# The second layer's down product computed as 15 products of block sums, with the sums of weights formed among keys and queries and the sums of activations formed in DRAM

## The chip, the cores and the metric

The kernel runs on one core of a Trainium2 chip. The metric is the device time of one launch in microseconds (us). The core has TensorE for matrix products (PE in the profile, with PEld for its weight loads), VectorE (DVE), ScalarE (ACT), GpSimd (POOL) and SyncE (SP), each with its own queue that runs in order, and 16 DMA engines that move data between DRAM and the on-chip memory. SP, ACT and POOL issue the DMAs.

## The reference

One inference step of a two-layer decoder over 1104 rows: 64 sample rows, 16 meta rows and 1024 prompt rows. The first layer mixes with an mLSTM, the second with a forgetting attention that reads one shared set of keys and values. Each layer ends with a SwiGLU feed-forward block, and this is the part that the change touches in the second layer:

```python
def swiglu(xn, w_gu, w_d):
    gu = xn @ w_gu
    return (jax.nn.silu(gu[..., :D_FF]) * gu[..., D_FF:]) @ w_d
...
h = h + swiglu(rmsnorm(h, prm['norm_ffn'][l]), prm['w_gate_up'][l], prm['w_down'][l])
```

The model width is 1024 and `D_FF` is 2816, which is 22 blocks of 128. All data is float32.

## The kernel before, in words

**Tiling.** Activations lie transposed, features on the 128 partitions and rows along the free axis, in three groups of rows `TS` of 336, 384 and 384 (`t` = 0, 1, 2; `SL` = 384 is the widest). A float32 operand is split into a high and a low part (`split`, L338 on ScalarE and L339 on VectorE), and a product is three matmuls, high·high, high·low and low·high (`mm3`, L266 to L268).

**Gate/up.** The gate/up product of both layers already runs as a scheme of 18 products and their block sums (`Unit`, L1505), one pass per 128 output columns: `Unit(x)` with even `x` makes gate values, with odd `x` up values, and the odd one multiplies them (L1524) and stores each finished 128-row block of the hidden activations to a DRAM buffer `hT[t]` from SP (L1525). Block numbers `f` run from 0 to 21; blocks 0 and 1 come from `direct`. The sums of gate/up weights are formed by POOL (`PairWeights.sums`, L108) one to two units ahead, and split by ScalarE and VectorE. In the loop over units only TensorE's order is written out by hand (`fixed()`); the other engines' order is chosen by a planner that simulates readiness.

**Down.** The loop over `seq` takes the three groups, two halves `z` of 512 output columns, and 11 pairs `c` of feature blocks: 66 steps. A step loads 256 x 512 weights from SP (`w_load`, L1629), splits them (`w_split`) and multiplies them for four output tiles `m`. Activations are loaded from `hT` by POOL (`h_load`, L1612) and split once per group and pair (`h_split`, used for both halves). Each output tile is added to the residual `H[t]` once, when its sum over all 22 blocks is done (L1480 is `add`, in this loop as in gate/up). TensorE's, VectorE's and ScalarE's order is written out here. `each` squares finished tiles for the final norm (`add_sq`; L411 on ScalarE, L413 on POOL, L639 and L641 for the last ones) and `final` transposes them (L1885), scales them (L1902) and stores the outputs.

**Keys and queries.** In `phase_b` the two projections `w_kvf` and `w_qo` are made in 256-column pieces, four each, over nine row tiles: 72 calls of `evac`, in which ScalarE copies (L2026) and squares the result and VectorE sums the squares (L2029). Three tiles later `then` scales a group (L2067) and `turn` transposes it on TensorE (L2040) and stores it from POOL (L2049). POOL also stores the keys (`out_rows`, L1989 to L1991). All orders here are the planner's.

**Queues and memory.** SP carries weight loads and the stores of `hT`; POOL's queue carries its additions and the DMAs that it issues. `order` is the hand-written order of TensorE, VectorE and ScalarE around the start of gate/up. `cw` holds the slots with gate/up weights, `cg` the tiles of gate/up alone.

## Time and profile before

| What | Value |
|---|---|
| Median of 3 runs | 2865.33 us (2863.34 to 2866.32) |
| Profiled execution, span from first to last instruction | 2855.2 us |
| TensorE busy | 2790.4 us, 98% |
| VectorE / ScalarE / GpSimd busy | 1724.8 / 1311.8 / 1018.3 us |
| Second layer's gate/up, from unit 2 | 2174 to 2572 us of the span |
| Second layer's down | 2572 to 2845 us |
| Keys and queries | 1378 to 1591 us |

For the profiled execution the span is the only time at hand; the runs' times are some 10 us longer, as they hold what lies before the first and after the last instruction. In the rows that follow, a group line gives the line of the kernel, engine, operation, output and inputs with their shapes and the count, then busy time and mean ns of one, then the idle time of the engine just before, and what ended most of it. A wait line gives who waited for whom: total us, times, the longest. A DMA line gives the issuing queue, count, size and median us from issue to landing.

### The profile page before, as it was taken

What the parts mean: (1) busy time and instruction counts of PE and PEld (TensorE: products, weight loads), DVE (VectorE), ACT (ScalarE), POOL (GpSimd) and SP (SyncE); (2) the same over time, 40 slices, a digit from 0 to 9 for tenths busy, and PEclk for the clock granted to TensorE, in tenths of its full rate; (3) what the DMA queues carried; (4) which work ended last, traced back from release to release, by engine and by line L of the source; (5) the groups of instructions that cost most, each with busy time, mean ns of one, the idle gap of its engine ahead of it and who ended that gap; (6) DMA issues with size and microseconds to landing.
All of it is one profiled execution on the core that took longest, in us unless ns stands there. A gap on an engine that the chain in (4) does not pass through costs nothing.

```text
span 2855.2 us, 53625 instructions
## 1 busy us (share of the span) xinstructions
PE 2790.4 (98%) x20485; PEld 2671.0 (94%) x20485; DVE 1724.8 (60%) x3478; ACT 1311.8 (46%) x2622; POOL 1018.3 (36%) x1495
## 2 busy tenths in 40 slices
PE   7999999999999999999999999999999999999999
PEld 7998989999999999999999888777999999999999
DVE  6044555887787755553355443777478777765553
ACT  6132464444444434443344544878244444443432
POOL 3022333075556311115352202554307656531210
PEclk9999999999999999999999999999999999999999
DMA  7057655132222275544443676442412222237652
GB/s 214 19 145 175 165 160 180 48 91 76 79 84 78 95 269 198 205 144 133 149 165 129 243 282 222 156 141 87 161 60 87 79 74 84 74 102 251 221 186 99
DMA packets 312444, 400.19 MB, mean 140 GB/s; under 512 B 28143, under 2 KB 235051, under 8 KB 311163
## 3 DMA queue, kind: packets, MB, share of 16 engines
q1 hardware_dynamic: 277234, 277.79, 30.7%
q0 software_dynamic: 33728, 118.38, 12.7%
q8 instruction: 161, 2.64, 0.4%
q10 hardware_dynamic: 1224, 0.60, 0.1%
q14 instruction: 97, 0.79, 0.1%
HBM read 299.92 MB, written 96.77 MB: 139 GB/s over the span
## 4 chain that ended last, share of the span: by engine, by line
PE 71%; DVE 9%; issue 4%; ACT 3%; DMA 2%; POOL 1%; DVEq 0%; ACTq 0%; SPq 0%; POOLq 0%
PE m L1505 24%; PE dps L266 6%; PE dps L268 6%; PE dps L267 6%; PE tmps L266 3%; PE tmps L268 3%; PE tmps L267 3%; PE sp L2597 2%; DVE slot L339 2%; PE pops L268 1%; PE pops L266 1%; PE pops L267 1%; PE op L2693 1%; PE bps L266 1%; DVE s L2606 1%
## 5 line engine op out<-in xcount | busy, mean ns | idle before, releaser
L339 DVE TENSOR_TENSOR slot<-slot,slot 128x1024 fp32r<-128x1024 f32 (+3 forms) x263 | 266.4, 1015 | 129.9 <-ACT slot L338 123.6
L338 ACT CAST slot<-slot 128x1024 fp32r<-128x1024 f32 (+3 forms) x263 | 206.8, 788 | 229.3 <-PE dps L267 91.3
L1505 PE MATMUL m<-x1h,slot 128*128 128x384 f32 x640 | 178.0, 338 | 2.4 <-DVE vA L1480 0.8
L1505 PE MATMUL m<-x0h,slot 128*128 128x336 f32 x640 | 167.0, 316 | 0.0
L413 POOL TENSOR_TENSOR ns<-ns,nq 128x384 f32<-128x384 f32 (+1 forms) x59 | 63.9, 1083 | 208.8 <-ACT nq L411 207.6
L1505 PE MATMUL m<-x2h,slot 128*128 128x384 f32 x480 | 135.8, 337 | 0.0
L1612 POOL DMA_DIRECT2D hr<-hT x60 | 32.6, 543 | 283.1 <-DVE T_2l L339 69.6
L108 POOL TENSOR_TENSOR slot<-Ht 128x256 f32<-128x256 f32 x80 | 74.9, 946 | 151.3 <-DMA Ht<-in_w_gate_up 147.0
L108 POOL TENSOR_TENSOR slot<-vA 128x256 f32<-128x256 f32 x80 | 74.2, 937 | 151.5 <-DMA vA<-in_w_gate_up 147.8
L339 DVE TENSOR_TENSOR slot<-Ht,slot 128x256 fp32r<-128x256 f32 (+3 forms) x101 | 84.8, 841 | 63.7 <-ACT slot L338 63.7
L339 DVE TENSOR_TENSOR slot<-vA,slot 128x256 fp32r<-128x256 f32 (+3 forms) x101 | 85.7, 850 | 61.7 <-ACT slot L338 61.7
L1505 PEld LDWEIGHTS m<-x1h,slot 128*128 128x128 f32 x640 | 117.1, 188 | 3.4 <-DVE vA L1480 1.2
L1505 PEld LDWEIGHTS m<-x0h,slot 128*128 128x128 f32 x640 | 113.3, 188 | 0.0
L1505 PE MATMUL m<-x1l,slot 128*128 128x384 f32 x320 | 107.8, 337 | 0.0
L1505 PE MATMUL m<-x0l,slot 128*128 128x336 f32 x320 | 101.0, 316 | 0.0
L1505 PE MATMUL m<-T_2h,slot 128*128 128x384 f32 x320 | 97.1, 344 | 3.0 <-ACT Ht L1511 0.9
L2629 ACT ACTIVATE s<-s,nb 128x272 f32<-128x272 f32 (+7 forms) x126 | 98.9, 787 | 0.2 <-POOL nb L2620 0.2
L1505 PE MATMUL m<-T_4h,slot 128*128 128x384 f32 x320 | 95.9, 340 | 0.0
L2664 ACT COPY th<-tp 128x768 f32<-128x768 f32 (+1 forms) x80 | 73.6, 921 | 46.4 <-PE tp L2656 25.9
L108 POOL TENSOR_TENSOR Ht<-Ht 128x512 f32<-128x512 f32 (+1 forms) x60 | 84.5, 1409 | 28.4 <-DVE wl1l L339 28.4
L108 POOL TENSOR_TENSOR vA<-vA 128x512 f32<-128x512 f32 (+1 forms) x60 | 84.5, 1409 | 27.5 <-DVE wl0l L339 27.5
L2029 DVE TENSOR_REDUCE ss<-sqb 128x4 f32<-128x256 f32 (+1 forms) x72 | 30.2, 419 | 101.3 <-ACT sqb L2028 100.4
(838 smaller groups left out, 10267.7 us busy)
## 6 DMA issues: line engine op xcount, KB each, us to landing
slot<-in_w_down SPq DMA_DIRECT2D x88, 512.0 KB, 4.4
wr<-in_w_down SPq DMA_DIRECT2D x42, 512.0 KB, 4.5
wraw<-in_w_in_a SPq DMA_DIRECT2D x40, 512.0 KB, 4.0
vA<-in_w_gate_up SPq DMA_DIRECT2D x40, 512.0 KB, 4.0
Ht<-in_w_gate_up SPq DMA_DIRECT2D x40, 512.0 KB, 4.1
hr<-hT POOLq DMA_DIRECT2D x46, 384.0 KB, 5.2
kp<-in_cache_k SPq DMA_DIRECT2D x32, 512.0 KB, 6.2
vp<-in_cache_v SPq DMA_DIRECT2D x32, 512.0 KB, 7.4
```

The lines of the kernel that those rows point to most:

```text
L108: self.net.nc.gpsimd.tensor_tensor(out=o, in0=a, in1=b, op=op)
L266: mm(ps, sh, mh, start=first, stop=False)
L267: mm(ps, sh, ml, start=False, stop=False)
L268: mm(ps, sl, mh, start=False, stop=last)
L338: self.nc.scalar.copy(hi, src)
L339: self.nc.vector.tensor_tensor(out=lo, in0=src, in1=hi.bitcast(F32), op=ALU.subtract)
L413: (nc.vector if x >= late else nc.gpsimd).tensor_tensor(out=s, in0=s, in1=sq, op=ALU.add)
L1505: nc.tensor.matmul(u.b[b][:, :n], w[p][:, k], x[q][:, k], start=new and k == i == 0, stop=k == 1 and i == 2, skip_group_check=True)
L1612: nc.gpsimd.dma_start(hraw[j], hT[t][:, 2 * c : 2 * c + 2])
L2597: nc.tensor.matmul(ps[z][:, :n], a[r, qs], b[r, at : at + n], start=(y == 0), stop=(y == 2))
L2629: nc.scalar.activation(ss[z, u], ss[z, u], AF.Exp, bias=nb[:, z : z + 1], accum_out=sm[:, u, z : z + 1])
L2664: nc.scalar.copy(th.rearrange("p x z (u h q) -> p h (x z u) q", h=2, q=64)[:, :, :n], pt[:, :, :n])
```

## The change

The hidden activations' first 21 blocks are taken as a 3 x 3 grid: three groups `k` of 7 feature blocks by three groups `t` of rows. The weights' first 21 blocks are a 3 x 2 grid: `k` by the two output halves `z`. The product of the two grids, 18 block products, is formed as 15 products, each of a signed sum of weight blocks with a signed sum of activation blocks, whose results are added to or subtracted from several output blocks. The 22nd block (`last`) is multiplied plainly inside some of them. The first layer keeps its down product (`plain`, now in `plain_down`).

- *Weights.* 4 of the 15 products read `w_down` as it is (`RAW`), 11 read sums (`MADE`) that `combine` forms in 14 rounds of loads (SP), additions (VectorE) and stores to DRAM (POOL). `evac` of keys and queries calls it one step at a time.
- *Activations.* `h_out` stores a finished block to all DRAM buffers that begin with it (`FIRST`), `h_minus` negates some tiles on ScalarE and stores them again (`MINUS`), and `h_add` adds one buffer to another by an accumulating DMA within DRAM that POOL issues (`ACCUMULATE` by unit, `LATER` for the last three blocks). In gate/up of the second layer POOL's order is now written out by hand too.
- *Down.* 62 steps of one or two blocks; each loads weights and activations (SP, the first five from POOL), splits both, and multiplies. A product's results stay in the four accumulators, the next may add to them with the fitting sign, and `evict` adds the state after a product to each output block that it names. Loads run eight steps ahead, splits three.
- *Around it.* Gate/up's tiles and weight slots are freed before down, whose tiles take their place; residuals are read back in halves at fixed steps; squares with index 4 and up are summed by VectorE in place of POOL; `order` is closed after the second of four parts of unit 2, in both layers.

```diff
+RAW = {1: (0, 0), 3: (0, 2), 5: (1, 0), 6: (1, 1)}
+MADE = (2, 11, 7, 12, 9, 8, 13, 10, 14, 4, 15)
+ACTS = {1: ("s1", 1), 2: ((1, 0), 1), 3: ("s3", 1), 4: ((1, 1), 1), 5: ("s5", 1), 6: ("s6", 1), 7: ("s7", -1),
+        8: ("s8", 1), 9: ("s9", 1), 10: ((0, 2), 1), 11: ("s11", -1), 12: ((2, 0), 1), 13: ("s13", 1), 14: ((0, 1), 1),
+        15: ((2, 2), 1)}
+FIRST = {(0, 0): ("s1", "s5"), (0, 1): ((0, 1), "s13", "s11"), (0, 2): ((0, 2), "s8"), (1, 0): ((1, 0),),
+         (1, 1): ((1, 1), "s3", "s9"), (1, 2): ("s6",), (2, 0): ((2, 0),), (2, 1): ((2, 1),), (2, 2): ((2, 2),)}
+MINUS = {(1, 0): "n10", (1, 2): "s7", (2, 0): "n20", (2, 1): "n21"}
+LATER = (("s5", "n20"), ("s13", (2, 0)), ("s3", (2, 0)), ("s11", "n21"), ("s9", (2, 2)), ("s3", (2, 1)), ("s11", (2, 2)),
+         ("s6", (2, 2)))
+ACCUMULATE = {9: (("s1", (0, 1), 0, 4), ("s5", (0, 2), 0, 4)), 11: (("s1", (0, 1), 4, 7), ("s5", (0, 2), 4, 7)),
+              15: (("s8", (1, 0), 0, 4), ("s6", (1, 0), 0, 4), ("s8", (1, 0), 4, 7)),
+              16: (("s6", (1, 0), 4, 7), ("s7", (0, 2), 0, 4), ("s1", "n10", 0, 4)),
+              17: (("s7", (0, 2), 4, 7), ("s7", (1, 1), 0, 4)), 18: (("s1", "n10", 4, 7), ("s7", (1, 1), 4, 7)),
+              19: tuple((a, b, 0, 4) for a, b in LATER[:4]), 20: tuple((a, b, 0, 4) for a, b in LATER[4:])}
+DOWN = ((2, 1, ((0, 0, 1),), None, True), (8, -1, ((0, 2, -1),), None, False), (10, 1, ((1, 2, 1),), None, False),
+        (5, -1, ((1, 0, -1),), (1, 0), False),
+        (12, 1, ((1, 0, 1), (1, 1, -1)), None, True), (14, 1, ((0, 1, 1),), None, False),
+        (1, -1, ((0, 0, -1),), (0, 0), False),
+        (13, 1, ((0, 0, 1),), None, True), (3, -1, ((0, 1, -1),), None, False), (11, 1, ((1, 1, 1),), (1, 1), False),
+        (4, 1, ((0, 2, 1),), None, True), (0, 1, ((0, 1, 1),), (0, 1), False),
+        (9, 1, ((0, 2, 1), (1, 1, 1)), None, True),
+        (15, 1, ((1, 1, -1),), None, True), (0, -1, ((1, 2, -1),), (1, 2), False),
+        (6, 1, ((1, 2, 1),), None, True), (7, -1, ((0, 2, -1),), (0, 2), False))
...
+                def each(t, m, x):
+                    if cb or t < 2 or x < KT - 2:
+                        self.add_sq(H, t, m, sp, x, KT - 1 if cb else 4)
...
+        def h_put(o, x, j):
+            n = min(hT[x].shape[2], o.shape[1])
+            nc.sync.dma_start(hT[x][:, j, :n], o[:, :n])
+
+        def h_out(o, f, t, c=None):
+
+            o = o[:, : size[t]]
+            if plain:
+                return nc.sync.dma_start(hT[t][:, f], o)
+            k, j = divmod(f, 7)
+            if k == 3:
+                return h_put(o, t, 0)
+            for x in FIRST[k, t]:
+                h_put(o, x, j)
+            if (k, t) in MINUS:
+                negs.append((c, o, MINUS[k, t], j))
+
+        def h_minus(cs):
+            for y in [y for y in negs if y[0] in cs]:
+                negs.remove(y)
+                _, o, x, j = y
+                nc.scalar.activation(o, o, AF.Copy, scale=-1.0)
+                h_put(o, x, j)
+
+        def h_add(x, y, a, b):
+            n = min(hT[x].shape[2], hT[y].shape[2])
+            nc.gpsimd.dma_start(hT[x][:, a:b, :n], hT[y][:, a:b, :n], accum_op=ALU.add)
...
+        steps = []
+        for p, s, ev, last, new in DOWN:
+            js = list(range(7)) if p else []
+            s = [s * (ACTS[p][1] if p else 1), s]
+            if last:
+                js.append(NF - 1)
+            parts = [js[:1]] * (len(js) % 2) + [js[x : x + 2] for x in range(len(js) % 2, len(js), 2)]
+            for x, ts in enumerate(parts):
+                n = size[0] if p in (1, 5) or p in (2, 12) and x else SL
+                steps.append((p, [s[j > 7] for j in ts], ts, last, n, new and x == 0, ev if x == len(parts) - 1 else None))
...
+        def x_load(e=nc.sync):
+            i = len(xraw)
+            if i == len(steps) or not place["tmp"]:
+                return False
+            p, _, ts, last, n, *_ = steps[i]
+            xraw[i] = place["tmp"].pop(0)
+            js = [j for j in ts if j < 7]
+            if js:
+                y = hT[ACTS[p][0]][:, js[0] : js[-1] + 1]
+                e.dma_start(xraw[i][:, : len(js), : y.shape[2]], y)
+                if y.shape[2] < n:
+                    nc.gpsimd.memset(xraw[i][:, : len(js), y.shape[2] :], 0.0)
+            if len(js) < len(ts):
+                e.dma_start(xraw[i][:, len(js), : size[last[1]]], hT[last[1]][:, 0])
+            return True
+
...
-        order.close()
-        with fixed():
+            if g % 2:
+                order.close()
+        with fixed(*(() if plain else (E.Pool,))):
...
+                    if g == 2 and not plain:
+                        for y in ACCUMULATE.get(x, ()):
+                            h_add(*y)
+                    if g == 3:
+                        if x + 2 < NF:
+                            weights.sums(x + 2, slice(0, 9))
+                    if x % 2 == 0 and g != 2:
+                        h_minus((("s1", "v2"), ("t4", "c15"), (), ("s2", "e"))[g])
...
+        if plain:
+            return plain_down(v)
+        dn = ExitStack()
+        with fixed(E.DVE, E.Activation, E.Pool, E.SP):
...
+            tail = u.tail()
+            next(tail)
             cg.close()
...
+            cw.close()
+            dp = dn.enter_context(self.pool(f"dn{l}"))
...
+            for y in range(5):
+                (x_load if y % 2 else w_load)(nc.gpsimd)
+            for y in range(2):
+                w_split(y)
+                x_split(y)
+            w_load()
+            w_load()
+            x_load()
+            x_load()
+            for _ in tail:
+                pass
+            h_minus(fs)
+            h_add(*LATER[0], 4, 7)
...
+            h_load(0, 0, 4)
+            h_load(2, 0, 4)
+            w_split(2)
+            x_split(2)
+            while len(wraw) < 7 and w_load():
+                x_load()
...
+            loads = {3: lambda: h_load(2, 4, 8), 6: lambda: h_load(0, 4, 8),
+                     9: lambda: h_load(1, 4, 8), 12: lambda: h_load(1, 0, 4)}
...
+            def evict(ev):
+                for m in range(4):
+                    for z, t, f in ev:
+                        h = H[t][:, 4 * z + m]
+                        tt(out=h, in0=h, in1=acc[m][:, : size[t]], op=ALU.add if f > 0 else ALU.subtract)
+                for z, t, f in ev:
+                    gone[z, t] = gone.get((z, t), 0) + 1
...
+            for i, (p, s, ts, last, n, lead, ev) in enumerate(steps):
+                w, x = wpart[i], xpart[i]
                 for m in range(4):
                     if lead:
...
+                        acc[m] = bank("dps", "f" if banks in (4, 5) else "d")
+                        banks += 1
+                    for k in range(len(ts)):
+                        for q, (a, b) in enumerate(((0, 0), (0, 1), (1, 0))):
+                            c = SL if lead and k == q == 0 else n
+                            nc.tensor.matmul(acc[m][:, :c], w[a][:, k, m * P : m * P + P], x[b][:, k, :c],
+                                             start=lead and k == q == 0, stop=k == len(ts) - 1 and q == 2,
+                                             skip_group_check=True)
+                for y, r in zip(("wh", "wl", "xh", "xl"), (*w, *x)):
+                    place[y].append(r)
+                if ev and (len(ts) == 1 or i == len(steps) - 1):
+                    evict(ev)
+                x_split(i + 3)
+                w_split(i + 3)
+                while len(wraw) <= i + 8 and w_load():
                     pass
+                while len(xraw) <= i + 8 and x_load():
+                    pass
+                if ev and len(ts) == 2 and i < len(steps) - 1:
+                    evict(ev)
+                if i in loads:
+                    loads[i]()
+                if i in range(4, 18, 2):
+                    h_add(*LATER[i // 2 - 1], 4, 7)
+                for _ in range(2 if p in (6, 7) else 1):
+                    next(norms, None)
+                for _ in range(99 if i == len(steps) - 1 else 2):
+                    if pend:
+                        pend.pop(0)()
+            for _ in end(fin, pp, 2):
...
+def combine(self, l, pool):
+
+    nc = self.nc
+    add = lambda o, a, b, op=ALU.add: nc.vector.tensor_tensor(out=o, in0=a, in1=b, op=op)
+    rows = self.I["w_down"][l][: 21 * P].rearrange("(k j p) n -> j p k n", k=3, p=P)
+    comb = self.dram.tile([len(MADE), 7 * P, 512], F32, name=f"wc{l}")
+    self.comb[l] = {p: comb[x] for x, p in enumerate(MADE)}
+    t = pool.tile([P, 15, 256], F32, name=f"wcs{l}")
+    w, o = t[:, :6], t[:, 6:]
+    for j in range(7):
+        for c in range(2):
+            at = lambda z: rows[j][:, :, 512 * z + 256 * c : 512 * z + 256 * c + 256]
+            put = lambda a, y: nc.gpsimd.dma_start(
+                comb[a, j * P : j * P + P, 256 * c : 256 * c + 256].rearrange("s p n -> p s n"), y)
+            nc.sync.dma_start(w[:, :3], at(0))
+            nc.sync.dma_start(w[:, 3], at(1)[:, 1])
+            nc.sync.dma_start(w[:, 4:], at(1)[:, ::2])
+            yield
+            yield
+            add(o[:, 0:2], w[:, 0:3:2], w[:, 1:6:4])
+            add(o[:, 2:4], w[:, 1:5:3], w[:, 3:6:2])
+            yield
+            add(o[:, 4], w[:, 2], w[:, 3])
+            add(o[:, 5:7], o[:, 0:2], w[:, 3:5])
+            yield
+            add(o[:, 7], o[:, 5], w[:, 4])
+            add(o[:, 8], o[:, 6], w[:, 0])
+            add(w[:, 1:4:2], w[:, 1:4:2], w[:, 2:6:3], ALU.subtract)
+            put(slice(0, 9), o)
+            put(slice(9, 11), w[:, 1:4:2])
+            yield
+
+
...
         behind = []
+        cm = ExitStack()
+        made = self.combine(1, cm.enter_context(self.pool("wcB")))
...
+                    next(made, None)
...
+        for _ in made:
+            pass
+        cm.close()
```

356 lines of the change are left out of this document (227 added, 129 removed).

## The prediction

> **What bounds the kernel now.** I read the page's busy shares and slices first, then the chain of work that ended last, then busy time by stretch for the three places that the change touches, then the groups, waits and DMA landings inside those stretches. All lines are of the kernel before.
>
> ```profile
> span 2855.2 us, 53625 instructions
> PE 2790.4 (98%) x20485; PEld 2671.0 (94%) x20485; DVE 1724.8 (60%) x3478; ACT 1311.8 (46%) x2622; POOL 1018.3 (36%) x1495
> ...
> PE   7999999999999999999999999999999999999999
> ...
> PEclk9999999999999999999999999999999999999999
> ...
> PE m L1505 24%; PE dps L266 6%; PE dps L268 6%; PE dps L267 6%; PE tmps L266 3%; PE tmps L268 3%; PE tmps L267 3%; PE sp L2597 2%; DVE slot L339 2%; PE pops L268 1%; PE pops L266 1%; PE pops L267 1%; PE op L2693 1%; PE bps L266 1%; DVE s L2606 1%
> ```
>
> TensorE is busy for 98% of the span, with a granted clock of nine tenths or more in every slice; the chain of last work is mostly its products, 24% of the span the gate/up products (L1505). Products taken away come off the time, unless something else is late where they stood. The places, one row each (PE, PEld, DVE, ACT, POOL busy with instruction counts, granted clock, DMA share, GB/s):
>
> ```profile
> 2572.00:2845.00 273.00, 273.00 (x1650) 272.73 (x1649) 132.65 (x141) 99.17 (x119) 39.34 (x50) 1.00 0.57 191
> 1378.00:1591.00 213.00, 213.00 (x1849) 213.00 (x1847) 108.97 (x255) 97.37 (x282) 85.64 (x133) 1.00 0.42 145
> 2174.00:2572.00 398.00, 395.95 (x2298) 392.51 (x2299) 301.94 (x478) 186.91 (x382) 217.71 (x217) 1.00 0.27 83
> ```
>
> First the second layer's down product, then keys and queries, then the second layer's gate/up from unit 2 on. In all three TensorE has no idle time worth a name, while VectorE is at 49%, 51% and 76% and the DMA engines at 0.57, 0.42 and 0.27 of their time. So the question is only which of the added work finds cover.
>
> **Part 1: the products removed.** Before, each of 3 token groups takes 2 output halves, 22 blocks of 128 features and 4 output tiles, three matmuls each (the split in high and low parts): 3·2·22·4·3 = 1584, one third of them 336 wide and the rest 384.
>
> ```profile
> 2575.00:2645.00 70.00, 70.00 (x457) 1.00 0.71 248
> 2660.00:2840.00 180.00, 174.93 (x993) 1.00 0.53 178
> 2572.00:2845.00 273.00, 267.66 (x1584) 1.00 0.57 191
> ```
>
> These are the same stretches for the products' own tile alone. The first holds 336-wide ones: 70.00/457 = 0.1532 us each. The second holds 384-wide ones, with the output's transposes between them: 174.93/993 = 0.1762 us. 528·0.1532 + 1056·0.1762 = 267.0, which is the third row's 267.66. After, 15 products of 7 blocks and 6 single blocks (the 22nd block, for each group and half) make 111 blocks of 12 matmuls. Products 1 and 5 are 336 wide with their 8 blocks each, 2 and 12 in all but their first block: 28 blocks narrow, 83 wide. 336·0.1532 + 996·0.1762 = 51.5 + 175.5 = 227.0. TensorE's saving is **40.0 us**; that term stands on counts and rows alone.
>
> **Part 2: weight sums among keys and queries.** Per round: three loads of 384, 128 and 256 KB on SP, seven additions of 2816 columns on VectorE, two stores of 1152 and 256 KB from POOL. There are 14 rounds, and a round advances one step after each of the 72 projections, five steps to a round.
>
> ```profile
> L2026 ACT COPY raw<-tmps x72: 353/373/377, 1379.5 to 1591.3; 128x256 f32<-128x256 f32 x64, 80x256 f32<-80x256 f32 x8
> L2029 DVE TENSOR_REDUCE ss<-sqb 128x4 f32<-128x256 f32 (+1 forms) x71 | 29.8, 419 | 101.1 <-ACT sqb L2028 100.2
> L339 DVE TENSOR_TENSOR slot<-slot,slot 128x512 fp32r<-128x512 f32 x37 | 27.2, 734 | 1.2 <-ACT slot L338 0.6
> L339 DVE TENSOR_TENSOR slot<-slot,slot 128x256 fp32r<-128x256 f32 x18 | 7.5, 419 | 0.7
> L1991 POOL DMA_DIRECT2D out_p_k<-raw x4 | 3.7, 916 | 0.4 <-issue 0.4
> slot<-in_w_qo_b SPq DMA_DIRECT2D x12, 512.0 KB, 4.4
> out_p_k<-raw POOLq DMA_DIRECT2D x4, 1024.0 KB, 5.5
> vD<-vst POOLq DMA_DIRECT2D x3, 1024.0 KB, 9.3
> POOL raw L2021 <- DMA out_p_k<-raw: 18.6, 4, 5.1
> 1600.00:1650.00 50.00, 48.97 (x541) 41.49 (x543) 21.00 (x66) 22.87 (x42) 7.32 (x13) 1.00 0.90 313
> ```
>
> VectorE: four additions of 512 columns at 734 ns and three of 256 at 419 make 4.2 us a round, 58.7 in all; 109 + 59 of 213 us is 79%, so as work it fits. DMA: 2176 KB a round, 31.2 MB in all, 146 GB/s on top of the stage's 145; the last row shows 313 GB/s moved at a share of 0.90, so this fits too, tightly. The order is what does not fit. The next round's loads overwrite rows that the second store still reads, so a round is one chain: load, add, issue, store. By rows: loads 4.9 (between 4.4 for 512 KB and 5.5 for 1024), additions 4.2 with a projection's reductions between them 5.5, two store issues on POOL 0.9 + 0.6 (the second an estimate from the first, as it is a quarter of the size), landing 6.9 (5.5 for 1024 KB alone, 9.3 for the second of two such stores issued together, hence 2048 KB; 1408 KB lies between). Sum 18.8 us. The program gives a round five projections of 213/72 = 2.96 us, 14.8. The ends: 14.7 with nothing between the additions and the nearest short landings (4.4 + 4.2 + 0.6 + 5.5), which is no delay; 22 with 9.3 us for the stores and 5.5 for the loads. Where a round is late by 4 us, VectorE's next addition waits in its queue with the reductions of later projections behind it. TensorE does not read VectorE's reductions; ScalarE empties its four banks, and VectorE sits idle for 101 us here already. But the transposes of finished groups read rows that VectorE scales, so lateness that adds up reaches TensorE there. POOL's own wait for a store in this stage (18.6 us over four, up to 5.1) cost TensorE nothing. Lower bound 0, upper 14·4.0 = 56 (100 with the longest landings every time). I take **8**, near the lower end, because the nearest row is a wait of that size that stayed free; rounds that end late run on beside the sample's attention.
>
> The Trainium skill's page "DMA: Bandwidth & Descriptors", section "Anatomy of one DMA — SWDGE (gpsimd) path", fits a transfer at 2.0 us plus bytes over 436 GB/s. By it 1408 KB land in 5.3 us and 768 KB in 3.8, the round takes 16.1, and the excess would be at most 14·1.3 = 18 us. This case's rows are slower than that fit (1024 KB: 5.5 against its 4.4), so I go by the rows.
>
> **Part 3: activation sums beside gate/up.** The stores of each finished block go to every sum that begins with it: 15 per block and 7 blocks, 28 negated copies and 3 for the last block, 136 stores instead of 66. POOL issues 30 accumulating transfers within DRAM, 22 here and 8 in the down product. ScalarE negates 28 tiles.
>
> ```profile
> hT<-Ht SPq DMA_DIRECT2D x28, 192.0 KB, 2.2
> L1527 ACT ACTIVATE ns<-ns 128x384 f32<-128x384 f32 x17 | 8.9, 524 | 27.4 <-DVE ns L1480 22.8 <-DVE ns L1481 4.6
> POOL slot L108 <- DMA Ht<-in_w_gate_up: 76.6, 17, 4.8
> hr<-hT POOLq DMA_DIRECT2D x23, 384.0 KB, 5.2
> vA<-hD POOLq DMA_DIRECT2D x4, 1536.0 KB, 9.5
> ```
>
> ScalarE: 28·0.52 = 15 us on 187 of 398. POOL: 22·0.9 = 20 us on 218, now in written order, with 76.6 us of waits for weights to absorb it. Stores: some 13 MB, 33 GB/s on 83. Each accumulation follows its blocks' stores by two units or more, so its wait is over when POOL reaches it. What is late next, if POOL is held, is the weight sums two units ahead. I take **2** (0 if POOL's waits absorb all, 20 if none). An accumulation's duration is in no row; the nearest are Pool-issued DRAM reads, 5.2 us for 384 KB and 9.5 for 1536, so 6.6 for 768 KB. The eight of units 19 and 20 would take 53 us; from their first issue to the down product's start are some 54 (a unit is 120 matmuls of 0.17 us, 21 us; 8 of unit 19, units 20 and 21, 4 of the last unit's rest).
>
> **Part 4: the start of down.** Its first five loads are issued by POOL, behind those accumulations; they wait until the gate/up operands that lay there are read. Twelve products of six matmuls stand after the last of these, 72·0.17 = 12 us, and load, cast and rest need 5 to 6. Before, TensorE goes from gate/up to down without a gap. I take **3** (0 to 27, the latter where an accumulation takes 10 us).
>
> **Part 5: down itself.** Every step now splits weights and activations: 62 steps (49 pairs, 13 single), and 76 evictions into H instead of 24, where the next product adds to the same bank.
>
> ```profile
> L339 DVE TENSOR_TENSOR slot<-slot,slot 128x1024 fp32r<-128x1024 f32 x42 | 55.9, 1334 | 49.1 <-ACT slot L338 49.1
> L339 DVE TENSOR_TENSOR x2l<-hr,x2h 128x768 fp32r<-128x768 f32 x8 | 7.6, 950 | 1.2 <-ACT x2h L338 1.2
> L1480 DVE TENSOR_TENSOR Ht<-Ht,dps 128x384 f32<-128x384 f32 x16 | 8.9, 554 | 37.7 <-PE dps L268 37.7
> L338 ACT CAST slot<-slot 128x1024 fp32r<-128x1024 f32 x41 | 43.0, 1050 | 91.6 <-PE dps L267 64.1 <-DMA slot<-in_w_down 25.0 <-PE dps L268 1.1
> L338 ACT CAST x2h<-hr 128x768 fp32r<-128x768 f32 x8 | 6.7, 833 | 2.8 <-DMA hr<-hT 2.8
> L1902 DVE SCALAR_TENSOR_TENSOR Ht<-fin,fr,gfin 128x512 f32<-128x512 f32 x16 | 11.1, 746 | 4.9 <-PE fin L1885 4.7
> SPq L1629 <- DVE slot L339: 176.5, 62, 11.8
> ```
>
> VectorE: 49·(1.33 + 0.95) + 13·(0.73 + 0.55) = 128, evictions 76·0.55 = 42, final scaling 18·0.75 = 13, squares 6 (those with index 4 and up move from POOL): 190 of 227 us, 84% where it was 49%. ScalarE: 49·(1.05 + 0.83) + 13·1.0 = 105 and 13 for squares, 52%. DMA: 29 MB of weights, 22 of activations, about the bytes of before in less time, 191·273/233 = 224 GB/s, below the 313 shown above. In a step that ends a product TensorE takes 24·0.176 = 4.2 us and VectorE 2.3 for the split and 2.2 for four evictions, 4.5; with two targets 6.7. The split runs three steps ahead, so VectorE starts early, and the excess is 0.3 at fifteen places and 2.5 at two: 9.5 at most, 0 where it starts early enough. I take **3**. SP's weight loads, which waited 176 us for free buffers, share their queue with the activations; they have eight steps' lead. That hand order ends two steps earlier in unit 2 of both layers I cost at nothing, as VectorE has 24% to spare there; if not, some 1 us a layer.
>
> **Part 6: the tail.**
>
> ```profile
> 2844.83 0.18 DVE Ht L1480
> ...
> 2845.30 0.56 DVE ns L641
> ```
>
> One eviction and one sum of squares lie between the last product and the end's scaling. Now four evictions stand ahead of the sums in VectorE's order; TensorE finishes tile by tile, so about **1** us.
>
> **Sum.** −40.0 + 8 + 2 + 3 + 3 + 1 = −23.0, against the profiled span of 2855.2: 2832. The median of the runs, 2865.3, is 10.1 above that span, which I leave as it is: 2842.
>
> **Rivals.** (a) *The round fits* (14.7 us, the lower end): keys and queries pay nothing, −31, 2834. For it: the short landings in the rows; against: 2.2 MB more each round lengthen them. Chance 0.20. It is where the page's fit, named above, points. (b) *Keys and queries run at the round's pace*, the case on the other side: the planner sets VectorE's additions by its own idea of a landing, each of 14 rounds is late by 4.0, and after one round's worth of slack (assumed) TensorE's transposes wait: 52 instead of 8, 2886. It turns the sign when the stage pays 31, at rounds of 17.3 us. For it: 18.8 against 14.8; against: TensorE's banks do not hang on VectorE. Chance 0.20. (c) *VectorE bounds down*: the excess of 9.5 comes in full, and half as much again from splits that then start late: 15 instead of 3, 2854. For it: 84%; against: three steps' lead. Chance 0.15. (d) *The accumulations are late*: at 10 us each, eight take 80 where 54 are there, so the first products wait some 27 instead of 3: 2866, no change, the case in which TensorE's saving is real and nothing comes of it. Chance 0.10, as no row shows such a transfer.
>
> **How the numbers follow.** My forecast has 0.35, (a) 0.20, (b) 0.20, (c) 0.15, (d) 0.10. A change of 0.2% (5.7 us) is about what can be told from none. Faster: forecast and (a) 0.55, (c) 0.14, (d) 0.03, (b) in part 0.02, together 0.74. Same: 0.01 + 0.03 + 0.03 = 0.07. Slower: (b) 0.15 and (d) 0.04, 0.19. Range: low end all costs at nothing, 2825; high end 2878, which leaves out most of (b). The forecast's own range is 2825 to 2855.
>
> **What the profile after would show.** Down's tile with 1332 matmuls in about 230 us; keys and queries at 213 us with TensorE without idle time and 14 rounds of additions at 4.2 us, their start 15 us apart (right) or 19 with TensorE idle before transposes (rival b); no gap at gate/up's end (d: ScalarE waiting for a DMA there); evictions that TensorE does not wait for (c: "PE waits for DVE H"). The prediction is wrong if the stretch of keys and queries grows by more than 15 us, or if a wait of SP or POOL for the accumulations ends at TensorE.

## The result and the profile after

The kernel after takes 2940.8 us (median of 5 runs, 2936.7 to 2944.5), the kernel before beside it 2863.3 us: a ratio of 1.0274, 95% interval 1.0261 to 1.0286. The change costs 2.7%. The forecast was 2842 us with a range of 2825 to 2878.

The first lines of the page, after:

```profile
span 2937.9 us, 53770 instructions
PE 2790.3 (95%) x20233; PEld 2663.9 (91%) x20233; DVE 1800.2 (61%) x3662; ACT 1327.0 (45%) x2676; POOL 1043.0 (36%) x1521
...
PE   7999989999999999999978899999999999987998
...
PEclk9999999999999999999989999999999999998999
```

TensorE is busy for as many microseconds as before (2790), although it runs 252 matmuls fewer, and for a smaller share. The row of PE now has slices at seven and eight tenths, at keys and queries (the 21st to 23rd) and about the start of down (the 36th and 37th), and PEclk has an 8 at the 21st and the 37th.

A timed run is about 2 us longer than its span, in all that are on record (2939.6 and 2937.9 for the one profiled here). The 10 us between median and profiled span of the kernel before are thus for the most part scatter: its span, 2855.2 us, is shorter than that of every timed run of that kernel on record (2855.7 to 2866.0).

The three places by stretch, in the same columns as before (us, PE, PEld, DVE, ACT, POOL busy with counts, granted clock, DMA share, GB/s): keys and queries, gate/up from unit 2, down; then the last stretch for down's tile alone (PE, PEld, DVE).

```profile
1389.00:1664.00 275.00, 234.24 (x1863) 231.94 (x1862) 156.74 (x364) 101.74 (x294) 111.37 (x163) 0.91 0.67 226
2243.00:2661.00 418.00, 400.67 (x2293) 393.74 (x2293) 291.75 (x473) 190.72 (x402) 232.23 (x240) 0.99 0.51 136
2661.00:2926.00 265.00, 242.02 (x1408) 239.71 (x1406) 169.57 (x228) 108.56 (x150) 24.56 (x24) 0.95 0.70 234
```

```profile
2661.00:2926.00 265.00, 234.06 (x1332) 230.92 (x1332) 38.38 (x76) 0.95 0.70 234
```

Keys and queries grew from 213 to 275 us and TensorE is idle for 41 of them; gate/up grew from 398 to 418 with 17 idle; down shrank from 273 to 265 only, with its 1332 matmuls as counted. For all kernels I use three stages of the profiled execution that meet without a gap: from the first copy of keys and queries to the first product of the attention's own gate behind them (`bps`; K), from there, over the attention, to gate/up's last product (G), from there to down's last product (D).

| | K | G | D |
|---|---|---|---|
| before | 216.4 | 973.9 | 274.3 |
| after | 276.0 | 996.2 | 264.5 |
| difference | +59.6 | +22.3 | -9.8 |

The other differences between the two spans (82.7 us in all) are +1.6 at the tail, +2.7 in the first layer's gate/up, +1.3 elsewhere ahead of K, and +5.0 in the first 440 us. That last part ranges from 434.2 to 440.8 us among the kernels below, none of which touches it, so it is scatter.

**Keys and queries.** Waits (who for whom, us, times, longest; `issue` is time in which nothing that the profile shows was waited for) and the landing of a round's large store, all after:

```profile
SPq L2142 <- DMA wc<-wcs: 84.2, 13, 9.7
DVE wcs L2131 <- DMA wcs<-in_w_down: 69.1, 11, 12.4
DVE wcs L2131 <- issue: 27.1, 4, 9.8
PE btp L2347 <- DVE raw L2374: 40.8, 12, 7.9
```

```profile
wc<-wcs POOLq DMA_DIRECT2D x14, 1152.0 KB, 6.6
```

SP's first load of a round waits for the store of the round before, VectorE's addition for the loads, and TensorE's transposes (`btp`) for the scaled rows (`raw`) that VectorE makes behind the additions. The rounds' first loads start 19.6 us apart in the mean, where the program has 14.8. One such wait in VectorE's order of time (start, us, instruction, and in brackets the idle time before it):

```profile
1503.62 0.42 DVE L2335 TENSOR_REDUCE ss<-sqb 128x4 f32<-128x256 f32 x1 [0.35 <-ACT sqb L2334]
1514.76 0.69 DVE L2131 TENSOR_TENSOR wcs<-wcs 128x512 f32<-128x512 f32 x1 [10.72 <-DMA wcs<-in_w_down]
1515.37 0.41 DVE L2335 TENSOR_REDUCE ss<-sqb 128x4 f32<-128x256 f32 x1
1515.70 2.42 DVE L2131 TENSOR_TENSOR wcs<-wcs 128x512 f32<-128x512 f32 x5
...
1519.72 0.95 DVE L2374 TENSOR_TENSOR raw<-raw,ss 128x768 f32<-128x768 f32 x1
```

VectorE stands 10.7 us at the first addition, and reductions and the scaling at 1519.7 come after it. What a gap does to TensorE, in stretches of 3 us:

```profile
1427.00:1430.00 3.00, 3.00 (x29) 3.00 (x28) 0.00 (x0) 0.00 (x0) 0.00 (x0) 1.00 0.88 279
1430.00:1433.00 3.00, 1.88 (x17) 1.68 (x15) 1.86 (x4) 0.74 (x4) 0.00 (x0) 1.00 0.10 36
1433.00:1436.00 3.00, 1.10 (x7) 1.13 (x7) 3.00 (x8) 0.92 (x4) 1.98 (x3) 0.68 0.32 131
1436.00:1439.00 3.00, 3.00 (x16) 3.00 (x15) 3.00 (x10) 1.55 (x4) 2.02 (x3) 0.50 0.95 324
1439.00:1442.00 3.00, 3.00 (x21) 3.00 (x20) 1.29 (x4) 0.66 (x2) 2.98 (x6) 0.68 0.97 340
1442.00:1445.00 3.00, 3.00 (x29) 3.00 (x28) 0.38 (x1) 1.01 (x4) 2.73 (x3) 1.00 1.01 349
```

TensorE is idle for 3.0 of the 6 us from 1430 to 1436, and from about 1434 to 1441 its granted clock is half (0.68 is a stretch that is part half, part full): 16 matmuls in 3 us where 29 are usual. So a wait is paid twice. Of the 59.6 us, 41 are idle time and 18 are slower products (234 us busy, where the stage's products take 216 at full clock). The Trainium skill's page "TensorE: Matmul & The Clock Gate", section "Part 1: The HAM clock gate", says that the clock is halved after an idle window of about 3.4 us and comes back after a busy one as long. The halving agrees; the slow time here, about 7 us, is longer than one such window.

**Gate/up and the start of down.** After: waits in gate/up, TensorE's wait in down and a wait of SP's queue at its start; landings from 2490 to 2660 us; down's start in stretches of 5 us; VectorE there in order of time.

```profile
ACT Ht L1542 <- DMA hT<-Ht: 37.5, 14, 6.4
PE m L1570 <- ACT ns L1576: 6.2, 6, 3.1
PE m L1570 <- ACT Ht L1576: 5.7, 8, 2.6
PE m L1570 <- ACT fs L1576: 4.4, 3, 3.0
PE dps L2098 <- DVE Ht L2079: 17.9, 2, 13.8
SPq L1523 <- ACT Ht L1542: 3.6, 1, 3.6
```

```profile
hT<-hT POOLq DMA_DIRECT2D x7, 768.0 KB, 11.8
hT<-Ht SPq DMA_DIRECT2D x18, 192.0 KB, 8.5
```

```profile
2678.00:2683.00 5.00, 3.67 (x24) 3.39 (x23) 0.00 (x0) 0.00 (x0) 0.00 (x0) 1.00 1.03 386
2683.00:2688.00 5.00, 0.00 (x0) 0.00 (x0) 2.16 (x2) 1.78 (x2) 0.00 (x0) 0.88 1.07 328
2688.00:2693.00 5.00, 0.00 (x0) 0.00 (x0) 0.27 (x1) 1.14 (x2) 0.00 (x0) 0.50 1.08 349
2693.00:2698.00 5.00, 2.54 (x8) 2.57 (x9) 5.00 (x8) 3.41 (x5) 0.00 (x0) 0.50 1.12 284
```

```profile
2685.17 0.96 DVE L1739 SCALAR_TENSOR_TENSOR dn1xl<-dn1tmp,dn1xh 128x768 fp32r<-128x768 f32 x1 [8.84 <-ACT dn1xh L1738]
2692.74 0.96 DVE L1739 SCALAR_TENSOR_TENSOR dn1xl<-x2l,dn1xh 128x768 fp32r<-128x768 f32 x1 [5.40 <-ACT dn1xh L1738]
2694.81 1.74 DVE L2079 TENSOR_TENSOR Ht<-Ht,dps 128x336 f32<-128x336 f32 x4
```

ScalarE negates in place (L1542) and must wait until the tile's first stores have been read out; these land after 8.5 us, where 2.2 were shown before. Its copies of finished products out of PSUM (L1576) stand behind it, and TensorE waits for those, 16 us in the three lines shown. At the start of down the DMA engines are full (share above 1), TensorE does nothing for some 14 us from 2682 and then starts at half clock. It waits for the first evictions (L2079); these come in VectorE's order behind two splits (L1739) for which VectorE stands 8.8 and 5.4 us, because ScalarE's casts wait for loads of activations that come late. SP's order seems to add to it (e12 below): its queue holds the last negated store (L1523), for which it waits 3.6 us, ahead of later loads of these.

### The profile page after: what moved, and what is told of

It is laid out like the page before. It is cut to its first block, busy times and chain, and to the rows that moved or that the text cites. A ratio compares the mean times of both kernels' runs of the same rounds, so it can differ in the third digit from the quotient of the medians.

```text
span 2937.9 us, 53770 instructions
## 1 busy us (share of the span) xinstructions
PE 2790.3 (95%) x20233; PEld 2663.9 (91%) x20233; DVE 1800.2 (61%) x3662; ACT 1327.0 (45%) x2676; POOL 1043.0 (36%) x1521
## 5 line engine op out<-in xcount | busy, mean ns | idle before, releaser
L365 DVE TENSOR_TENSOR slot<-slot,slot 128x256 fp32r<-128x256 f32 (+2 forms) x219 | 208.4, 953 | 84.2 <-ACT slot L364 76.6
L364 ACT CAST slot<-slot 128x256 fp32r<-128x256 f32 (+2 forms) x219 | 160.7, 735 | 151.8 <-PE m L1570 82.9
L2098 PE MATMUL dps<-dn1xh,dn1wh 128*128 128x384 f32 (+1 forms) x444 | 150.3, 339 | 20.4 <-DVE Ht L2079 17.9
L2098 PE MATMUL dps<-dn1xl,dn1wh 128*128 128x384 f32 (+1 forms) x444 | 149.3, 336 | 1.0 <-DVE dn1xl L365 1.0
L2098 PE MATMUL dps<-dn1xh,dn1wl 128*128 128x384 f32 (+1 forms) x444 | 149.1, 336 | 0.0
L365 DVE TENSOR_TENSOR slot<-Ht,slot 128x256 fp32r<-128x256 f32 (+2 forms) x100 | 82.4, 827 | 84.8 <-ACT slot L364 84.7
L134 POOL TENSOR_TENSOR slot<-Ht 128x256 f32<-128x256 f32 x80 | 68.7, 869 | 159.3 <-DMA Ht<-in_w_gate_up 129.4
L2131 DVE TENSOR_TENSOR wcs<-wcs 128x512 f32<-128x512 f32 (+1 forms) x98 | 52.0, 571 | 96.5 <-DMA wcs<-in_w_down 69.1
L2098 PEld LDWEIGHTS dps<-dn1xh,dn1wh 128*128 128x128 f32 x444 | 85.8, 193 | 21.7 <-ACT dn1xh L1738 14.0
```

The source lines that it names most:

```text
L134: self.net.nc.gpsimd.tensor_tensor(out=o, in0=a, in1=b, op=op)
L364: self.nc.scalar.copy(hi, src)
L365: self.nc.vector.tensor_tensor(out=lo, in0=src, in1=hi.bitcast(F32), op=ALU.subtract)
L2098: nc.tensor.matmul(acc[m][:, :c], w[a][:, k, m * P : m * P + P], x[b][:, k, :c], start=lead and k == q == 0, stop=k == len(ts) - 1 and q == 2,
L2131: add = lambda o, a, b, op=ALU.add: nc.vector.tensor_tensor(out=o, in0=a, in1=b, op=op)
```

## The experiments

Times are medians, ratios against the kernel before on the same chip; all edits are to the kernel after (2940.8) unless said otherwise. The stages of each:

| | time | ratio (95%) | K | G | D |
|---|---|---|---|---|---|
| e1 | 2923.2 | 1.0205 (1.0186 to 1.0224) | 257.5 | 1001.1 | 264.3 |
| e2 | 2931.9 | 1.0247 (1.0228 to 1.0266) | 264.8 | 999.5 | 265.8 |
| e3 | 2881.5 | 1.0061 (1.0043 to 1.0078) | 216.5 | 1000.1 | 265.5 |
| e4 | 2939.8 | 1.0270 (1.0253 to 1.0287) | 275.7 | 997.5 | 264.8 |
| e5 | 2936.1 | 1.0256 (1.0229 to 1.0283) | 270.7 | 1003.5 | 263.3 |
| e6 | 2969.7 | 1.0377 (1.0355 to 1.0400) | 303.0 | 1004.8 | 264.2 |
| e7 | 2910.6 | 1.0166 (1.0149 to 1.0183) | 275.1 | 979.8 | 254.0 |
| e8 | 2926.0 | 1.0222 (1.0205 to 1.0239) | 275.8 | 983.9 | 263.4 |
| e9 | 2928.2 | 1.0229 (1.0212 to 1.0246) | 264.4 | 996.4 | 266.3 |
| e10 | 2939.6 | 1.0271 (1.0254 to 1.0288) | 275.3 | 998.6 | 263.5 |
| e11 | 2932.7 | 1.0244 (1.0227 to 1.0261) | 275.3 | 997.3 | 255.4 |
| e12 | 2914.9 | 1.0182 (1.0165 to 1.0199) | 264.8 | 999.6 | 248.9 |
| e13 | 2882.9 | 1.0073 (1.0056 to 1.0090) | 216.4 | 1000.9 | 265.6 |
| e14 | 2949.3 | 1.0300 (1.0276 to 1.0325) | 276.1 | 1005.4 | 263.4 |
| e15 | 2923.7 | 1.0214 (1.0197 to 1.0231) | 276.0 | 998.1 | 246.2 |
| e16 | 2877.4 | 1.0052 (1.0035 to 1.0068) | 216.5 | 1012.4 | 250.0 |
| e17 | 2865.9 | 1.0008 (0.9999 to 1.0017) | 217.7 | 996.4 | 247.4 |
| e18 | 2857.4 | 0.9981 (0.9972 to 0.9990) | 216.5 | 990.6 | 248.2 |

Where a kernel leaves a stage's work as it is after, K scatters from 275 to 276 us, G from 996 to 1005 and D from 263 to 266.

### Keys and queries: e3, e1, e2, e5, e6, e9, e13

**e3**, no weight sums (`made = iter(())`, and the products read rows of `w_down`):

> The weight sums are left out: no loads, additions and stores among keys and queries, and the second layer's down product reads rows of w_down as they are where it read sums. Theory: keys and queries are back at 212 us, the kernel 2941 - 60 = 2881 us, and the other two losses (gate/up +22, start of down +30) stay as they are. Rival (the stretch is longer for another reason, such as a different order of the work): the kernel within 10 us of 2941.

2881.5, K back at 216.5: the whole loss of this stage comes from the weight sums, and G and D keep theirs.

**e1**, blocks of their own for the subtractions:

```diff
-            add(w[:, 1:4:2], w[:, 1:4:2], w[:, 2:6:3], ALU.subtract)
+            add(d, w[:, 1:4:2], w[:, 2:6:3], ALU.subtract)
```

> The two subtractions of a round are written into two blocks of their own, so that the next round's first loads wait for the additions alone and no longer for the store. Theory (one chain of store, load, additions): a round falls from 19.6 us to about 13 and so to the program's own pace of 14.8; keys and queries take 212 to 225 us instead of 271, the kernel 2882 to 2895 us. Rival 1 (VectorE's additions stand in its order ahead of what the products need, and wait there for the loads, whatever the loads waited for): a round stays above 17 us, the kernel above 2915. Rival 2 (31 MB of traffic and 59 us of VectorE's work are what keys and queries pay): the kernel within 10 us of 2941.

18 of 60 us came back. A round's loads now start 10 to 20 us apart, 13.4 in the mean, and the last by 1564 us, where the last round's started at 1640 in the kernel after, and yet K stays at 257: the chain was not the whole cause. The time is in the range of rival 1, though its rounds were to stay above 17 us and did not.

**e2**, two sets of blocks (`w, o = sets[c]`):

> Two sets of blocks in turn, so that a round's loads wait for the additions and the store of the round but one before. Chain theory: as with the blocks for the subtractions, within 8 us of that run, keys and queries 212 to 220 us, the kernel about 2882 to 2890. Rival 1 (VectorE waits in order for the loads): this run gains 20 us or more over the one with separate blocks, since the loads are there a round earlier. Rival 2 (traffic and VectorE's work): the kernel within 10 us of 2941.

9 us only; fewer than e1 gave. By its number this is rival 2, which e13 below rules out.

**e5**, e1 with additions of one column (`out=o[..., :1]`):

> The run with blocks for the subtractions (2923 us, keys and queries 257 us), and each of a round's seven additions computes only the first of its columns: the waits, the loads and the stores stay, VectorE's 4.2 us a round fall to about 0.5. What the sums hold is left out. Theory (what is left over of the loss after the chain is VectorE's own time and its place in the order): keys and queries 212 to 222 us, the kernel 2885 to 2893. Rival 1 (traffic of 31 MB beside the weight loads): within 8 us of 2923. Rival 2 (VectorE waits at its additions for the loads): 2905 to 2923, since those waits stay.

No gain; the kernel is 13 us slower than e1. The stretch of keys and queries, and what VectorE waits for:

```profile
1384.00:1654.00 270.00, 228.02 (x1865) 226.46 (x1865) 123.20 (x365) 101.36 (x294) 111.89 (x166) 0.92 0.67 231
```

```profile
DVE wcs L2131 <- DMA wcs<-in_w_down: 55.6, 16, 8.2
DVE wcs L2131 <- DMA wc<-wcs: 22.0, 4, 7.7
```

VectorE is busy for 123 us instead of 157 and still waits 78 us, in the two lines shown, at additions that do next to nothing. So its own time is unlikely to be what the stage pays; why this kernel is slower than e1 was not looked into, and its time lies in none of the three ranges.

**e6**, e1 with the additions on GpSimd (`nc.gpsimd.tensor_tensor`):

> The run with blocks for the subtractions, with all its additions on GpSimd instead of VectorE (GpSimd's sums of 128x512 took 0.9 to 1.5 us in gate/up, so a round's 2816 columns take about 7 us there, 98 us in all). Theory (VectorE's order is what the products wait for): keys and queries below 230 us, the kernel 2885 to 2900. Rival (the waits move along: GpSimd's queue also issues the stores of keys and queries, whose buffers ScalarE needs): the kernel 2915 or more.

K 303: the rival. ScalarE waited 119 us for the stores of keys and queries (`kDh`, `qDh`), which GpSimd issues behind the additions.

**e9**, e2 with each round's loads a round ahead in the program:

> Two sets of blocks in turn, as in the run that gained 9 us, but a round's three loads stand in the program ahead of the round before's additions, a whole round (14.8 us by the program's pace) before their own. Theory (what is left of the loss in keys and queries is VectorE standing at an addition whose load has not landed, 6 to 8 us at a time, with the normalisations behind it; its own time costs nothing, since thin additions gained nothing): keys and queries 216 to 232 us, the kernel 2881 to 2900 us. Rival (traffic of 31 MB beside the other loads): keys and queries stay above 255, the kernel above 2918.

2928.2, near e2's, and by its number the rival. SP issued these loads at the same times as in e2, within 1 us: the build's planner orders SP and VectorE by its own idea of readiness, and the place in the program did not bind it. So this run did not test what it was meant to, and its expectation failed for a reason that stood in the description of the kernel before.

**e13**, e9 with each third of the additions tied to the reduction just made:

```diff
+        nc.vector.tensor_copy(o[:, 0, :1], self.tick)
+        nc.vector.tensor_copy(o[:, 2, :1], self.tick)
         add(o[:, 0:2], w[:, 0:3:2], w[:, 1:6:4])
...
+                    self.tick = ss[:, i, :1]
                     next(made, None)
```

> As the run with loads a round ahead, and each third of a round's additions first copies one column of the sums of squares that VectorE has just reduced into the block that it will write: so the additions cannot stand in VectorE's order ahead of the products' progress, and a round takes 14.8 us or more, its loads having been issued a round before. Traffic and additions are unchanged. Theory (VectorE standing in its order at additions that wait for loads): keys and queries 216 to 232 us instead of 264, the kernel 2882 to 2900. Rival (31 MB of traffic and 59 us of VectorE's work): keys and queries above 250, the kernel above 2915.

2882.9, K 216.4, as before the change and as without any sums:

```profile
1385.00:1601.00 216.00, 216.00 (x1868) 215.99 (x1867) 173.76 (x451) 102.36 (x293) 112.26 (x165) 1.00 0.83 281
```

TensorE is busy for 216.00 of 216.00 us at full clock, beside 281 GB/s at a DMA share of 0.83 and VectorE at 80% (174 of 216). All loads, additions and stores are still there. VectorE waits for no load of the sums any more; its longest waits in the stage are these, for ScalarE's squares:

```profile
DVE ss L2350 <- ACT sqb L2349: 30.2, 24, 2.6
```

This settles the main question of the stage: neither the traffic nor VectorE's work costs anything; what cost 60 us was additions that stood in VectorE's order before their loads had landed. The ties were not tried with the one set of blocks of the kernel after, so how much of the cure needs the second set stays open.

### Gate/up: e4, e7, e8, e10, e14

**e4**, negations into one tile of their own (`nc.scalar.activation(ng, o, ...)`), the last two into free tiles:

> ScalarE writes the 28 negated activations into a tile of their own, one in each quarter of a unit, instead of over the activation that is being stored; the last two go into tiles that are free by then. Theory (gate/up's loss is ScalarE's wait for the stores, 37.5 us in 14 waits by the trace, which holds up its copies out of PSUM): gate/up recovers 12 to 22 us, and the start of down up to 5 more, the kernel 2915 to 2928 us. Rival (the accumulations that GpSimd issues between its sums, and their traffic, make the units slow): 0 to 5 us, the kernel 2935 to 2941.

No change, but no test either: ScalarE waited 33.9 us in 13 waits for that tile's own last store.

**e7**, no accumulations (`h_add` does nothing):

> The 30 accumulating transfers are left out, and with them the activation sums; all stores stay. Theory (their traffic and GpSimd's order make gate/up lose 22 us and fill the DMA engines at the start of down): gate/up recovers 10 to 22, the start of down 10 to 25, the kernel 2896 to 2920 us. Rival (the stores, 136 against 66 on SP's queue ahead of the weight loads, and the first loads of down behind them): the kernel 2930 or more.

30 us came back, 16 in G and 10 in D, as the theory said. The stores' landing, and the waits of ScalarE and TensorE in gate/up, to compare with the lines of after above:

```profile
hT<-Ht SPq DMA_DIRECT2D x21, 192.0 KB, 2.2
```

```profile
ACT Ht L1542 <- DMA hT<-Ht: 9.6, 9, 1.3
PE m L1570 <- ACT Ht L1576: 1.3, 5, 0.5
```

Without accumulations beside them the stores land in 2.2 us again, ScalarE's wait falls from 37.5 to 9.6 us, and TensorE's wait for these copies from 5.7 to 1.3.

**e8**, no negations (`h_put(o, x, j)` alone):

> The 28 negations on ScalarE are left out, and with them the sign of what is stored; the stores stay, and nothing on ScalarE waits for a store any more. With the negations in a tile of their own ScalarE still waited 34 us in 13 waits, for that tile's own store, so that run could not tell. Theory (ScalarE's waits make gate/up slow): gate/up recovers 12 to 22 us, the kernel 2918 to 2928. Rival (they are hidden, accumulations or stores are the cause): the kernel 2936 to 2941.

15 us came back, 12 in G, although stores still took 6.8 us to land. Together with e7 this speaks for one mechanism: accumulations make stores late, and the negations turn late stores into a wait ahead of PSUM copies. Taking either away gives more than half of G's loss.

**e10**, negations a quarter of a unit later in the program, the last two into free tiles:

```diff
-                        h_minus((("s1", "v2"), ("t4", "c15"), (), ("s2", "e"))[g])
+                        h_minus(((), ("s1", "v2"), ("t4", "c15"), ("s2", "e"))[g])
```

> The negations of s1, v2, t4 and c15 stand a quarter of a unit (about 5 us) later, and the last two are written into tiles that nothing stores from. Theory (accumulations make a store land 6 us late, the negation in place waits for it, and ScalarE's copies out of PSUM stand behind): gate/up recovers 6 to 14 us and the start of down up to 5, the kernel 2922 to 2934. Rival (the wait only moves: the negated tile's own store is then late for the copy that reuses the tile): the kernel 2936 to 2944.

No change, as the rival had it; ScalarE still waited 30.5 us in 13 waits. Its order is the planner's too, so a later place in the program need not be a later place on the engine, and the run tells nothing of the theory.

**e14**, negations on GpSimd, the last two on ScalarE into free tiles:

> GpSimd negates in place instead of ScalarE, with the waits for the stores then on GpSimd, in whose order the sums of the weights two units ahead stand behind; the last two negations stay on ScalarE and go into tiles that nothing stores from. Theory (the wait costs because ScalarE's copies out of PSUM stand behind it): gate/up recovers 8 to 14 us, the start of down up to 6, the kernel 2921 to 2933. Rival (GpSimd's sums are late instead, since it has no room for 30 us of waits): 2936 to 2955.

Nothing came back. The time is 9 us longer, but the two intervals overlap, and G, 1005, is at the edge of its scatter. The time is in the rival's range, though not for its reason: TensorE's waits are for ScalarE, with copies that reuse a tile waiting for its late negation and store:

```profile
ACT Ht L1581 <- DMA hT<-Ht: 22.8, 5, 13.4
```

### The start of down: e11, e15

**e11**, loads of H and accumulations of down tied to the steps:

```diff
+            def pace(i):
+                y = xpart[i + 3][0].bitcast(F32)[:, 0, :1]
+                nc.gpsimd.tensor_tensor(out=zz, in0=y, in1=y, op=ALU.add)
...
                 if i in loads:
+                    pace(i)
                     loads[i]()
```

> Four of the six loads of H and seven accumulations of down each stand on GpSimd behind a small sum that reads the split activations three steps ahead, so that they start with the steps instead of all at 2670 to 2713 us; nothing is left out. Theory (the DMA engines are full at the start of down, share above 1.0 from 2680 to 2740, and the first products' loads share them): the start of down recovers 8 to 20 us, the kernel 2921 to 2933. Rival (the loads are late because they stand behind gate/up's last stores on SP's queue): the kernel 2936 to 2944.

8 us came back, in D, which is 9 us shorter: the low end of the theory.

**e15**, e11 with the last negations into free tiles and fewer loads ahead (5 in place of 7 at first, then `i + 5 + i // 6`):

> As the paced run (2933 us), the last two negations into tiles that nothing stores from, and loads for 5 steps instead of 7 to 8 are issued ahead at the start. Theory (the first products' loads share the DMA engines with loads for later steps): the start of down gains 5 to 12 us more, the kernel 2918 to 2928. Rival (the first loads are late by when they are issued): within 4 us of 2930, or slower by the steps that then wait.

9 us more, D 246.2, inside the theory's range, but mostly not by its cause. e12 below has the paced start and the free tiles, all loads ahead as in after, and its D is already 248.9; so having fewer loads ahead is worth 2.7 us, within D's scatter. Most of the 9 us go with the free tiles, which alone gave nothing in D (e4, e10, e14: 263 to 265). TensorE's wait for evictions falls from 17.9 to 6.8 us:

```profile
PE dps L2109 <- DVE Ht L2090: 6.8, 2, 6.2
```

### Together: e12, e16, e17, e18

**e12**, e9, e10 and e11 in one:

> The three edits together. If each cures a loss of its own, their gains add: 2941 - 50 - 12 - 13 = 2866 us, between 2845 and 2890, level with the kernel before; what would be left then are the rest of gate/up's loss and of the start of down. If they share one cause (the DMA engines' load), the sum is smaller: above 2890.

2914.9, a miss, since two of the three did not act; D gained 16, more than e11's 9 alone. What it has beyond e11 there is e10's free tiles for the last two negations: SP no longer waits for ScalarE ahead of its first loads, where that wait was 4.6 us in e11.

**e16**, e13, e14 and the paced start:

> Tied additions, negations on GpSimd, and the paced start of down. If the three causes are separate and these cures act: 2941 - 48 - 12 - 14 = 2867, between 2850 and 2890. If keys and queries keep their loss, 2900 to 2915.

2877.4, inside the range expected, but with only two of the three cures: K as in e13, D 250, G at 1012 the worst of all, with e14's edit.

**e17**, e13, e15 and tied negations:

```diff
+                    nc.scalar.activation(mone, tied[:, :1], AF.Copy, scale=0.0, bias=-1.0)
+                nc.scalar.activation(g, o, AF.Copy, scale=-1.0 if tied is None else mone)
...
+                    if x % 2 == 0 and g == 1:
+                        h_minus(("s1", "v2", "t4", "c15"), u.b[2])
+                    if x % 2 == 0 and g == 2:
+                        h_minus(("s2", "e"))
```

> Tied additions in keys and queries; negations of s1, v2, t4 and c15 in place, each scaled by a -1 that ScalarE makes from the second quarter's last product, those of s2 and e into a tile of their own; the paced start of down with 5 steps of loads ahead. Without gate/up's part the cures add up to 2941 - 58 - 17 = 2866 us. Theory (gate/up's loss is ScalarE standing at negations that wait for late stores): gate/up recovers 8 to 14 us more, the kernel 2848 to 2860, faster than the 2863 before by 0.1 to 0.5%. Rival (the accumulations' traffic makes gate/up slow by other ways, such as late weight loads): 2862 to 2870.

2865.9, just the sum of the cures without gate/up's part: the rival's number. The negations no longer wait for stores, but copies that reuse a tile do:

```profile
ACT Ht L1580 <- DMA hT<-Ht: 17.5, 5, 6.1
```

**e18**, e17 with gate/up's accumulations spread, one at a time (two pairs near the end started together all the same):

```diff
-                    if g == 2 and not plain:
-                        for y in ACCUMULATE.get(x, ()):
+                    if g != 1 and not plain:
+                        for y in ACCUMULATE.get(x, ())[(0, 0, 1, 2)[g] : (1, 0, 2, 3)[g]]:
```

> As the run with all cures (2866 us), but gate/up's 22 accumulations start one at a time, in the first, third and last quarters of the units 9 to 20, at most three to a unit, where the middle units had none and the last four had two to four at once. Theory (a store lands late when several accumulations share the DMA engines, and ScalarE, the weight loads and so TensorE wait for it): gate/up recovers 6 to 14 us of its 20, the kernel 2852 to 2860, 0.1 to 0.4% faster than before. Rival (each accumulation delays what it meets, alone or not): within 4 us of 2866.

2857.4, ratio 0.9981 (0.9972 to 0.9990): faster than the kernel before by 5 us, 0.2%, and by 83 than the change as it was made. ScalarE's wait at copies, and the landing of single accumulations:

```profile
ACT Ht L1581 <- DMA hT<-Ht: 1.1, 1, 1.1
```

```profile
hT<-hT POOLq DMA_DIRECT2D x3, 672.0 KB, 7.2
```

The copies' wait is 1.1 us where it was 17.5. G is 990.6, still 17 us above before, and D 248.2, 26 below; so 26 of the 40 us saved arrive there. What holds the rest was not tried.

## Why the prediction was wrong

**Part 1 was right.** 1332 matmuls, as counted; they are busy 234 us instead of the forecast 227, and most of the difference goes with the slower clock behind the start's gaps (granted clock 0.87 up to 2740 us).

**Part 2 failed, in the price that it chose between its two ends: 8 us against 59.6.** The sizes were right: the round was put at 18.8 us and measured 19.6, the work was said to fit as work (79% of VectorE, traffic tightly), and e13 showed both at no cost. The text then priced the excess at 8 us "near the lower end, because the nearest row is a wait of that size that stayed free". That row was POOL's, behind whose wait TensorE lost nothing; the wait in question was VectorE's, behind which the scaling of `raw` stands. Rival (b) came nearest, the planner's idea of a landing included. But the chain of store, load and additions, from which it and the forecast are priced, is not the whole: with the chain cut (e1) 41 of the 60 us stayed, and they went when the additions were tied to the reductions, with two sets of blocks (e13). Its 52 us were to be idle time, and TensorE's was 41; that they come near the loss of 59.6 is in part luck. What argued against it, that TensorE's banks do not hang on VectorE, was true and beside the point, since the transposes do. What neither the forecast nor a rival had is the clock, 18 of the 59.6.

**Part 3 failed: 2 us against 22** (and against more in most kernels with the same gate/up, by G's scatter). It asked whether ScalarE and POOL have time for the added work, and they had. It named what is behind a late POOL, but not what is behind the negation: a wait for a store of the same tile, on the engine that empties PSUM. And it took the stores' 2.2 us as given, where accumulations in flight beside them made 8.5 (e7, e8).

**Part 4 failed: 3 us against about 28.** D lost 30 us (40.0 saved, 9.8 gained), and Part 5's share of it is small. The price came from the five loads alone. Six loads of residuals and eight accumulations, which POOL issues as soon as its queue lets it, started within some 45 us, beside the loads eight steps ahead; spreading them gave back 9 us (e11). The last two negations, which wait in place for their stores and hold up SP's first loads, were in no price either; with free tiles for them D fell by 5 to 7 us more (e16 and e12 against e11). Rival (d) foresaw a first product that waits some 27 us, and accumulations of 10 us or more, but named their end as the cause; more than them stood together.

**Part 5 held, and rival (c) did not come:** after 2740 us no product of down waits for VectorE, and TensorE waits for it 1.5 us in all, at the output's transposes. **Part 6** held, 1.6 against 1. **The hand order** that ends two steps earlier, costed at nothing or "some 1 us a layer", may be the 2.7 us of the first layer's gate/up; that was not tried by itself.

So the sum of costs that was to eat into 40 us was 17, and is 59.6 + 22.3 + 30.2 + 1.6 + 4.0 = 117.7, beside 5.0 of scatter.

**The fit.** The 1152 KB stores landed in 6.6 us, where the fit of the Trainium skill's page "DMA: Bandwidth & Descriptors", section "Anatomy of one DMA — SWDGE (gpsimd) path", gives 4.7; going by the rows was right, and the round still took longer than either sum. The fit is one for transfers that GpSimd issues, so it bears on the round's stores and not on its loads, which SP issues. Nor did it point at rival (a), as the prediction has it: by its own sum the round takes 16.1 us, which is above 14.8.

## What to carry to other kernels

When work is put beside other work, a free engine is not cover enough: ask which instruction will stand at a wait, and what is behind it on that engine. Where a planner sets the order, moving a line in the program may move nothing; a data dependency on the work that should come first does (e9 against e13: 264 and 216 us for the same loads and additions). A wait of TensorE is paid a second time in clock, here with nearly half as much again (18 us beside 41).

## What the hardware did that I had not expected

- An accumulating transfer within DRAM lands after 7.2 us for 672 KB when one runs at a time, and after 11 to 12 us for 672 to 768 KB where two to four run together; beside them a store of 192 KB takes 8.5 us instead of 2.2.
- A pause of 3 us (1430 to 1436, above) cost TensorE some 7 us at half clock behind it; behind one of 3.7 us, up to 1563, it was some 3.4.
